# Filling a 1 MB DRAM scratch with 128 copies of a bias vector: from four SBUF partitions, or DRAM to DRAM with rows outermost

## Chip, core and metric

The kernel runs on one core of a Trainium2 chip. The metric is device time in microseconds (us) of one execution; lower is better.

## The reference, cut to what matters

Two networks of two layers each run one after the other on 256 tokens of width 1024 in fp32. The first block is a recurrent branch and a sliding-window attention, a cross attention and a SwiGLU feed-forward; the second is a differential attention beside a long convolution (Hyena). The part that this case touches is the position bias of the differential attention, which depends on the distance between key and query alone:

```python
bucket = t5_bucket(k_pos[None, :] - q_pos[:, None])      # 32 buckets
bias = rel_bias[bucket].astype(jnp.float32).transpose(2, 0, 1)   # 4 heads
logits = jnp.einsum('bhcqd,bhckd->bhcqk', q_blk, kt).astype(jnp.float32)
p = jax.nn.softmax(logits + bias[None, :, None], axis=-1)
```

## The kernel before

**The weight stream.** Almost all the work is `x @ w` with weights from DRAM. `run_stream` takes the weights in chunks of 1 MB. A chunk is loaded into one of three `raw` buffers (`NRAW`, L211, issued on SP's queue). Each chunk is used in two halves. A half is split into a high and a low part: ScalarE copies it to `wh` (L229) and VectorE subtracts to get `wl` (L231). The splits run four halves ahead of TensorE (`NW`). The matmuls (L361) of `fm` and `tm` take the split halves. A `raw` buffer is loaded again once its second half is split.

**The feed-forward (`ffn`).** In layer 1 of the first block it runs 11 rounds. A round takes two chunks of `ffn_wi` (matmuls into `fm`, then `silu` at L1004 and L1005) and one chunk of `ffn_wo` (matmuls into `ff`).

**Order of issue.** The program's order on TensorE and SP is written out by a planner in the file (`self.t`, the table `L`), which interleaves side chains between the halves of the weight stream. GpSimd (POOL) issues the small transfers in the chains' order.

**The bias chain (`load_bias`).** It is the tail of the chain `prep_co`, spawned just before the feed-forward of layer 1. One matmul of the bucket table with `rel_bias` gives, for each of the four heads, a vector of 512 values by distance, in four partitions (`vec`, L1224). POOL then writes 128 copies of it to a DRAM scratch `flat` (`scr`, L1226), 4 heads x 128 copies x 2 KB, 1 MB in all. Two POOL loads (L1232) read the scratch back with a row step of 511 instead of 512, so that each of the 128 partitions gets the vector shifted by one position (`bias`, 384 columns of two heads each). VectorE adds `bias` to the scores in `diff_co` (L1446) in the second block.

Of the kernel before, what the change touches and what calls it, by code (L numbers as in the profile page):

```python
# [13 lines left out]
F32 = mybir.dt.float32  # L14
# [6 lines left out]
P = 128  # L21
D = 1024
KD = D // P
S = 256
# [14 lines left out]
LATE = ((0, 0), (1, 0), (1, 1))  # filters whose products fill gaps of the tensor engine  # L39
# [5 lines left out]
# estimated time from the issue of a stage until its results are there, ns  # L45
# [10 lines left out]
def shape_constants():  # L56
    f32 = np.float32
    c = {}
    pos = np.arange(S, dtype=f32)
    inv = np.power(f32(500000.0), -np.arange(0, 16, 2, dtype=f32) / f32(16)).astype(f32)  # L60
    ang = (pos[:, None] * inv[None, :]).astype(f32).astype(np.float64)
    c["c_rope"] = np.concatenate([np.cos(ang), np.sin(ang)], axis=1).astype(f32)
    q = P + np.arange(P)[:, None]
    k = np.arange(S)[None, :]
    c["c_mask"] = np.where((k <= q) & (k > q - P), 0.0, NEG).astype(f32)
    # odd frequencies of length 2 S: g = f + 1/2 for f < P; those of 2 P - g follow from the
    # sums over even and odd positions
    t = np.arange(S).reshape(P, TB).T.reshape(TB, P, 1)
    th = 2.0 * np.pi * ((t * (2 * np.arange(P) + 1)) % 1024) / 1024.0
    fwd = np.concatenate([np.cos(th), -np.sin(th)], axis=2)  # L70
    c["c_fwd"] = np.ascontiguousarray(fwd.transpose(1, 0, 2)).astype(f32)
    c["c_inv"] = np.ascontiguousarray(
        fwd.reshape(TB, P, 2, P).transpose(3, 0, 2, 1)).reshape(P, TB, 2 * P).astype(f32)
    rel = np.arange(512) - 255
    n = np.abs(rel)
    large = np.full(512, 8)
    for edge in (12, 16, 23, 32, 46, 64, 91):
        large = large + (n >= edge)
    bucket = np.where(rel > 0, 16, 0) + np.where(n < 8, n, large)
    c["c_bucket"] = (np.arange(32)[:, None] == bucket[None, :]).astype(f32)  # L80
    tl = np.linspace(0.0, 1.0, S, dtype=f32)[:, None]
    fb = np.linspace(1e-4, 15, 16, dtype=f32)[None, :]
    za = (f32(2.0 * math.pi) * np.arange(S, dtype=f32)[:, None] * fb / f32(S)).astype(np.float64)
    z = np.concatenate([tl, np.cos(za), -np.sin(za)], axis=1).astype(f32)
    c["c_z"] = np.ascontiguousarray(z.reshape(P, TB, 33).transpose(2, 1, 0).reshape(33, S))
    c["c_nt"] = np.ascontiguousarray(-tl.reshape(P, TB))
    return c


class Chunk:  # L90
    """One weight transfer of [P, a, b], used in two halves (by column or by row)."""
# [12 lines left out]
class Net:  # L104
    def __init__(self, ctx, tc, a):
        self.tc, self.nc, self.a = tc, tc.nc, a
        self.const = ctx.enter_context(tc.tile_pool(name="const", bufs=1))
        self.wraw = ctx.enter_context(tc.tile_pool(name="wraw", bufs=NRAW))
        self.wspl = ctx.enter_context(tc.tile_pool(name="wspl", bufs=NW))
        self.slots = ctx.enter_context(tc.tile_pool(name="slots", bufs=NSLOT))  # L110
        self.sm = ctx.enter_context(tc.tile_pool(name="sm", bufs=2))
        self.ps = ctx.enter_context(tc.tile_pool(name="ps", bufs=4, space=PSUM))
        self.pa = ctx.enter_context(tc.tile_pool(name="pa", bufs=4, space=PSUM))
        self.dr = ctx.enter_context(tc.tile_pool(name="dr", bufs=1, space=bass.MemoryType.DRAM))
        self.n = 0
        self.first_hi = None
        self.start = True
        # splits of weights wait while a norm holds the vector engine, then queue behind .defer
        self.pause, self.defer = False, None
        self.t = 0.0  # L120
        self.chains, self.bg = [], []
        nc = self.nc
        self.ident = self.const.tile([P, P], F32, name="ident")
        make_identity(nc, self.ident)
        self.mhalf = self.const.tile([P, 4], F32, name="mhalf")
        nc.vector.memset(self.mhalf, -0.5)

    # ------------------------------------------------------------------ order of issue
    # Chains are generators that issue a stage and yield the time until the next one can start;
    # the weight stream runs between their stages.  # L130
# [14 lines left out]
    def pump(self):  # L145
        """issues the stages that are due"""
# [6 lines left out]
    def idle(self, until=None):  # L153
        """tensor engine has nothing to do: background stage, or let time pass"""
# [23 lines left out]
    def run_stream(self, gen):  # L178
        """items: Chunk, or a function to call when its turn comes"""
# [95 lines left out]
    def pin(self):  # L275
        """queues the block's work behind the latest split of weights"""
# [5 lines left out]
    # ------------------------------------------------------------------ tiles  # L282
# [10 lines left out]
    def fmt(self, name, n=2, dt=F32):  # L293
        """feature-major tensor, 4 chunks of [P, S] to a tile"""
# [27 lines left out]
    def tmp(self, shape, name="s", dt=F32):  # L322
        """short-lived: released by the stage that takes it"""
# [3 lines left out]
    def keep(self, shape, name="s", dt=F32):  # L327
        """lives over a few stages of a chain"""
# [19 lines left out]
    # ------------------------------------------------------------------ building blocks  # L348
# [26 lines left out]
    def fm(self, w, c0, ncols, x, evac, kc=KD):  # L375
        """chunks of x() @ w, feature-major; evac(pair, psum)"""
        step = 2048 // kc
        nm = step // 2 // P
        for c in range(c0, c0 + ncols, step):
            box = {}  # L380

            def half(h, wh, wl, c=c, box=box):
                xx = x()
                for i in range(h * nm, h * nm + nm):
# [4 lines left out]
                    # parts of one kind together: the others may still be on their way  # L389
# [16 lines left out]
    def tm(self, w, c0, ncols, x, evac):  # L406
        """chunks of x() @ w, token-major, 256 columns each; evac(chunk, block, psum)"""
        for c in range(c0, c0 + ncols, 256):
# [4 lines left out]
            def part(h, tb, wt, ps):  # L413
                xx = x()
                t = slice(tb * P, tb * P + P)
                if self.start:
                    # the lo part of the weights comes last
# [38 lines left out]
    def to_fm(self, src, x, scale=None):  # L456
        """chain: token-major [P, D] per block -> split feature-major x; gain and bias"""
# [31 lines left out]
    def load_x(self, src, name, n=1):  # L489
        """token-major loads, in n column parts"""  # L490
# [7 lines left out]
    # ------------------------------------------------------------------ block 1  # L498
# [58 lines left out]
    def ln_evac(self, t, h, n=256, f=1.0, gb=None, pause=False):  # L557
        """evac for tm: t = f * ALPHA * h + psum, psum being f times the branch, and its
        statistics; normalises a full block, with gain and bias if given"""
# [38 lines left out]
    def ln_co(self, l, i, t, hT):  # L598
        """chain: normalised t -> hT (split feature-major), then t *= gain, t += bias"""
# [8 lines left out]
    def swa_co(self, l, s):  # L608
        """chain: s.q, s.kv token-major -> s.ya feature-major split"""
# [111 lines left out]
    def conv4(self, l, s):  # L721
        """evac: stores the padded pair; a chain convolves it"""
# [23 lines left out]
    def gates(self, l, s):  # L746
        """chunks of the block-diagonal gate products"""
        nc, a = self.nc, self.a

        def half(h, which, wh, wl):  # L750
# [6 lines left out]
            # ig holds tanh(x / 2) = 2 sigmoid(x) - 1  # L757
# [22 lines left out]
    def rnn_co(self, l, s):  # L780
        """chain: gates r, ig and conv output xc -> hidden states times gelu(gr), split"""
# [19 lines left out]
        # the factor 1/2 of the input gate  # L801
# [23 lines left out]
    def merge(self, wa, wb, xa, xb, s, kc, before_b):  # L825
        """s.mg = 2 (sigmoid(a) * (xa @ wa) + sigmoid(b) * (xb @ wb)), feature-major split;
        s.sa, s.sb hold tanh(a / 2), tanh(b / 2) = 2 sigmoid - 1"""
# [26 lines left out]
    def mixer(self, l, s):  # L854
        """s.h, s.hT -> s.t (normalised token-major sums)"""
# [73 lines left out]
    def cross_co(self, s, hp):  # L929
        """chain: one head pair of cross attention up to transposed probabilities"""  # L930
# [41 lines left out]
    def cross_out(self, s):  # L972
        """attention-weighted values, feature-major split"""
# [93 lines left out]
    def block1(self, s):  # L1067
# [14 lines left out]
        for l in range(DEPTH):  # L1082
            last = l == DEPTH - 1
            # first half of the layer
# [58 lines left out]
    # ------------------------------------------------------------------ block 2  # L1143
    def load_block2(self):
# [16 lines left out]
        # the last layer's columns twice: the halves of its output take the hi and the lo part  # L1161
# [27 lines left out]
    def load_dft(self):  # L1189
        """transforms by parity of the position: [P, parity, cos | -sin], hi and lo"""  # L1190
# [13 lines left out]
    def dft_pair(self, part, src, alloc, name):  # L1204
        """cos (0) or -sin (1) sums of src over even and odd positions"""
# [8 lines left out]
    def load_bias(self):  # L1214
# [9 lines left out]
        nc.vector.tensor_copy(vec, ps)  # L1224
        flat = self.dr.tile([4, (P + 1) * 512], F32, name="scr")
        nc.gpsimd.dma_start(flat[:, :P * 512].rearrange("h (p r) -> h p r", r=512),  # L1226
                            vec[:, None, :].to_broadcast([4, P, 512]))
# [34 lines left out]
    def filter_piece(self, l, o, res):  # L1262
        """spectrum of the two-sided filter of order o, scaled for the inverse transform"""
# [86 lines left out]
    def filter_end(self, o, raws, res):  # L1350
        """sums and differences of the sums over even and odd positions"""
# [10 lines left out]
    def spectrum(self, u, flt, box):  # L1362
        """forward transform of u (token-major split [P, parity, 512]) times the filter's, as
        the operands of the inverse sums over even and odd positions"""
# [32 lines left out]
    def inverse(self, box, par, name):  # L1397
        """positions of one parity, token-major"""
# [29 lines left out]
    def diff_co(self, s, tb):  # L1428
        """chain: one query block of differential attention -> s.ya feature-major split"""
# [105 lines left out]
    def hyena_co(self, s, conv):  # L1535
        """chain: both long convolutions -> s.yh feature-major split"""
# [50 lines left out]
    def pre_co(self, l, s):  # L1587
        """chain: rms norm of s.x -> s.hT feature-major split"""
# [120 lines left out]
    def prep_co(self):  # L1709
        """chain: position biases and filters of block 2"""  # L1710
# [24 lines left out]
    def build(self, what, out):  # L1735
        """what: 1 or 2 for one block alone, 3 for both"""
# [45 lines left out]
```

## Time and profile before

| what | us |
|---|---|
| median of 3 runs | 1610.3 (1603.89 to 1612.5) |
| span of the profiled execution, first to last instruction (the only time given for it) | 1607.2 |
| TensorE busy in it | 1530.2 (95%) |
| mean granted TensorE clock in it | 0.978 |

All stretches are in microseconds from the start of the profiled execution's span. PE is TensorE's matmuls, DVE VectorE, ACT ScalarE, SPq the queue of the sync engine. [...] The transfers of one core run on 16 DMA engines; POOL's go through the queue q0, SP's through q1.

### The profile page before, as it was taken

How to read it: one execution, taken by the hardware profiler on the slowest of the kernel's cores; microseconds unless marked ns; L12 is line 12 of the kernel's file. 1: busy time of each engine (PE TensorE's matmuls, PEld its weight loads, DVE VectorE, ACT ScalarE, POOL GpSimd, SP SyncE). 2: the span in 40 equal slices, each digit the busy share in tenths (PEclk: the TensorE clock that was granted, in tenths of full speed). 3: DMA queues.
4: the chain of work that ended last, by engine and by line, in shares of the span. 5: the costliest groups of instructions: out<-in, count | busy, mean ns of one | idle time of the engine just before them, and what ended most of it. 6: DMA issues, size and time to landing. Idle time of an engine off the chain costs nothing. (4 is left out here: it accounts for less than half of the span.)

```text
span 1607.2 us, 28221 instructions
## 1 busy us (share of the span) xinstructions
PE 1530.2 (95%) x11740; PEld 1459.3 (91%) x11740; DVE 1135.2 (71%) x1646; ACT 879.3 (55%) x1406; POOL 138.1 (9%) x176
## 2 busy tenths in 40 slices
PE   8999999998999989999989899985999999999997
PEld 7889999998999989899989789975799899898997
DVE  5867677667664587767686776533798978797965
ACT  5789444534444446795446456622645565654753
POOL 5001002002000030010030210000000000000000
PEclk9999999999999999999999999996999999999999
DMA  8444654544555554446555375645454346354452
GB/s 274 132 132 146 223 185 157 172 156 157 165 178 187 186 165 134 130 145 211 196 162 192 105 236 186 202 119 171 131 162 158 123 141 197 132 163 157 133 170 79
DMA packets 228240, 263.10 MB, mean 164 GB/s; under 512 B 6367, under 2 KB 213497, under 8 KB 228112
## 3 DMA queue, kind: packets, MB, share of 16 engines
q1 hardware_dynamic: 221808, 246.43, 47.2%
q0 software_dynamic: 6304, 14.86, 3.8%
q8 instruction: 92, 1.51, 0.4%
q14 instruction: 36, 0.29, 0.1%
HBM read 259.17 MB, written 2.10 MB: 163 GB/s over the span
## 5 line engine op out<-in xcount | busy, mean ns | idle before, releaser
L231 DVE TENSOR_TENSOR wl<-raw,wh 128x1024 fp32r<-128x1024 f32 x464 | 570.1, 1232 | 312.0 <-ACT wh L229 309.2
L229 ACT ACTIVATE wh<-raw 128x1024 fp32r<-128x1024 f32 (+1 forms) x465 | 489.5, 1056 | 477.2 <-PE fm L361 271.3
L361 PE MATMUL fm<-h2h,wh 128*128 128x256 f32 x704 | 174.7, 289 | 25.0 <-ACT wh L229 23.8
L361 PE MATMUL fm<-h2l,wh 128*128 128x256 f32 x704 | 175.1, 290 | 9.9 <-DVE h2l L351 9.9
L361 PE MATMUL fm<-n2h,wh 128*128 128x256 f32 x640 | 176.6, 286 | 1.4 <-ACT n2h L350 1.4
L361 PE MATMUL fm<-n2l,wh 128*128 128x256 f32 x640 | 175.0, 284 | 0.0
L361 PE MATMUL fm<-n2h,wl 128*128 128x256 f32 x640 | 174.5, 283 | 0.0
L361 PE MATMUL fm<-h2h,wl 128*128 128x256 f32 x704 | 173.9, 288 | 0.5 <-DVE wl L231 0.5
L361 PEld LDWEIGHTS fm<-h2h,wh 128*128 128x128 f32 x704 | 126.9, 197 | 29.7 <-ACT wh L229 24.2
L361 PEld LDWEIGHTS fm<-h2l,wh 128*128 128x128 f32 x704 | 126.1, 198 | 11.5 <-DVE h2l L351 11.5
L361 PEld LDWEIGHTS fm<-h2h,wl 128*128 128x128 f32 x704 | 125.7, 197 | 0.8 <-DVE wl L231 0.8
L361 PEld LDWEIGHTS fm<-n2h,wh 128*128 128x128 f32 x640 | 119.9, 192 | 3.5 <-ACT n2h L350 1.9
L361 PEld LDWEIGHTS fm<-n2l,wh 128*128 128x128 f32 x640 | 119.8, 192 | 0.8 <-DVE n2l L351 0.8
L361 PEld LDWEIGHTS fm<-n2h,wl 128*128 128x128 f32 x640 | 119.9, 192 | 0.2
L361 PE MATMUL tm<-wh,mgl 128*128 128x256 f32 x256 | 72.5, 283 | 0.7 <-DVE mgl L351 0.7
L361 PE MATMUL tm<-wh,mgh 128*128 128x256 f32 x256 | 72.4, 283 | 0.0
L361 PE MATMUL tm<-wl,mgh 128*128 128x256 f32 x256 | 72.4, 283 | 0.0
L361 PE MATMUL fm<-h3h,wh 128*128 128x256 f32 x256 | 71.2, 288 | 0.0
L361 PE MATMUL fm<-xTh,wh 128*128 128x256 f32 x256 | 70.9, 287 | 0.0
L361 PE MATMUL fm<-h3l,wh 128*128 128x256 f32 x256 | 70.3, 285 | 0.0
L361 PE MATMUL fm<-h3h,wl 128*128 128x256 f32 x256 | 70.2, 284 | 0.0
L361 PE MATMUL fm<-xTl,wh 128*128 128x256 f32 x256 | 69.8, 283 | 0.0
(440 smaller groups left out, 4185.7 us busy)
## 6 DMA issues: line engine op xcount, KB each, us to landing
raw<-in_w_in_dram SPq DMA_DIRECT2D x89, 1024.0 KB, 5.3
raw<-in_ffn_wi_dram SPq DMA_DIRECT2D x44, 1024.0 KB, 5.1
raw<-in_ffn_wo_dram SPq DMA_DIRECT2D x22, 1024.0 KB, 5.0
raw<-in_w_out_dram SPq DMA_DIRECT2D x16, 1024.0 KB, 5.1
raw<-in_ckv_w_dram SPq DMA_DIRECT2D x16, 1024.0 KB, 5.2
raw<-in_w_br_attn_dram SPq DMA_DIRECT2D x8, 1024.0 KB, 5.1
raw<-in_w_br_rnn_dram SPq DMA_DIRECT2D x8, 1024.0 KB, 5.3
raw<-in_cq_w_dram SPq DMA_DIRECT2D x8, 1024.0 KB, 5.2
```

Of the source, the lines that this page charges most:

```text
L229: hi_ins = self.nc.scalar.activation(hi[:, i:i + q], s[:, i:i + q], AF.Copy)
L231: lo_ins = self.nc.vector.tensor_tensor(lo, s, hi.bitcast(F32), op=ALU.subtract)
L361: self.nc.tensor.matmul(out, lhsT=l, rhs=r, start=start, stop=stop)
```

## The change

The vector is first written once to a DRAM tile `one` (8 KB). The 128 copies are then made by a second transfer, also issued by POOL, from that tile to the scratch. Its access pattern has the 128 copies as the outermost dimension and the four heads inside; before, the four heads (partitions) were outermost. The contents of the scratch and all that reads it are the same.

```diff
         vec = self.tmp([512], "vec")[:4, :]
         nc.vector.tensor_copy(vec, ps)
+
+        one = self.dr.tile([4, 512], F32, name="row")
+        nc.gpsimd.dma_start(one, vec)
         flat = self.dr.tile([4, (P + 1) * 512], F32, name="scr")
-        nc.gpsimd.dma_start(flat[:, :P * 512].rearrange("h (p r) -> h p r", r=512),
-                            vec[:, None, :].to_broadcast([4, P, 512]))
+        nc.gpsimd.dma_start(flat[:, :P * 512].rearrange("h (p r) -> p h r", r=512),
+                            one[None, :, :].to_broadcast([P, 4, 512]))
```

The rest of the diff replaces comments and docstrings by blank lines.

## Rows read from the trace of the kernel before

**Rows 1.** The page: share of the span, and granted clock in 40 slices.

```profile
PE 1530.2 (95%) x11740; PEld 1459.3 (91%) x11740; DVE 1135.2 (71%) x1646; ACT 879.3 (55%) x1406; POOL 138.1 (9%) x176
...
PEclk9999999999999999999999999996999999999999
```

**Rows 2.** PE's waits, 1060 to 1260: in total, times, longest (us).

```profile
PE fm L361 <- ACT wh L229: 23.8, 1, 23.8
```

**Rows 3.** PE in order of time: start, duration, what, [idle before <- releaser].

```profile
1078.97 0.39 PE L361 MATMUL ff<-wh,al 128*128 128x512 f32 x1
1103.15 0.80 PE L361 MATMUL fm<-h2h,wh 128*128 128x256 f32 x2 [23.79 <-ACT wh L229]
...
1105.01 0.63 PE L361 MATMUL fm<-h2l,wh 128*128 128x256 f32 x2
...
1109.63 0.28 PE L361 MATMUL fm<-h2l,wh 128*128 128x256 f32 x1
```

**Rows 4.** ACT in order of time, the splits and the rounds' silu.

```profile
1069.13 0.58 ACT L1004 ACTIVATE silu<-fm 128x512 f32<-128x512 f32 x1
1102.04 2.00 ACT L229 ACTIVATE wh<-raw 128x1024 fp32r<-128x1024 f32 x2 [32.33 <-DMA raw<-in_ffn_wi_dram]
...
1113.42 0.58 ACT L1004 ACTIVATE silu<-fm 128x512 f32<-128x512 f32 x1
1115.34 1.06 ACT L229 ACTIVATE wh<-raw 128x1024 fp32r<-128x1024 f32 x1 [1.34 <-PE fm L361]
...
1130.40 0.58 ACT L1004 ACTIVATE silu<-fm 128x512 f32<-128x512 f32 x1
```

**Rows 5.** Two windows: length, busy by engine, clock, DMA share, GB/s.

```profile
1080.00:1090.00 10.00, 0.00 (x0) 0.00 (x0) 0.00 (x0) 0.00 (x0) 0.00 (x0) 0.61 0.25 31
...
1104.00:1108.00 4.00, 3.59 (x17) 3.59 (x18) 4.00 (x6) 2.57 (x4) 0.00 (x0) 0.50 0.71 261
```

**Rows 6.** DMA queues, 1072 to 1096: packets, MB, share of 16 engines.

```profile
q0 software_dynamic: 148, 0.61, 23.6%
q1 hardware_dynamic: 148, 0.15, 1.8%
```

**Rows 7.** DMA issues: count, KB each, us from issue to landing.

```profile
scr<-vec POOLq DMA_DIRECT2D x1, 1024.0 KB, 44.0
raw<-in_ffn_wi_dram SPq DMA_DIRECT2D x1, 1024.0 KB, 43.3
...
raw<-in_ffn_wi_dram SPq DMA_DIRECT2D x44, 1024.0 KB, 5.1
...
rb<-in_rel_bias_dram POOLq DMA_DIRECT2D x1, 0.5 KB, 2.9
```

**Rows 8.** SP's queue in order of time, from 1056.

```profile
1058.59 6.60 SPq L211 DMA_DIRECT2D raw<-in_ffn_wi_dram  x2
```

**Rows 9.** DMA queue, 1044 to 1050: weight loads alone.

```profile
q1 hardware_dynamic: 1231, 1.24, 64.0%
```

**Rows 10.** POOL in order of time, 1055 to 1150.

```profile
1057.73 1.13 POOL L1226 DMA_DIRECT2D scr<-vec  x1 [83.76 <-DVE vec L1224]
...
1147.00 1.00 POOL L454 TENSOR_TENSOR rs<-rs,mhalf 128x1 f32<-128x1 f32 x1 [43.27 <-DVE rs L450]
```

**Rows 11.** The use of bias: duration min/median/max, first and last start.

```profile
L1446 DVE SCALAR_TENSOR_TENSOR dsc<-ds,bias x16: 674/680/685, 1253.9 to 1513.8; 128x512 f32<-128x512 f32 x16
```

**Rows 12.** DMA, 924 to 930: POOL loads of DRAM rows copied to 128 partitions.

```profile
q0 software_dynamic: 278, 1.00, 61.3%
...
raw<-in_ffn_wo_dram SPq DMA_DIRECT2D x1, 1024.0 KB, 12.5
```

**Rows 13.** DMA queue, 1596 to 1604: stores of the output to DRAM.

```profile
q1 hardware_dynamic: 576, 1.05, 35.0%
```

**Rows 14.** All waits of PE, 915 to 960: total, times, longest.

```profile
PE fm L361 <- DVE h2l L351: 5.0, 4, 1.8
PE fm L361 <- ACT h2h L350: 1.2, 1, 1.2
```

## Prediction

> **What bounds the kernel now.** I read the page first. TensorE is busy 95% of the span and its granted clock is nine tenths or more in every slice but one, around 1085 to 1125, where it falls to six tenths [rows 1]. Almost everywhere the time is matmuls in a row, and nothing this change touches makes them shorter. So the question is what happens in that one slice, and whether the bias chain has to do with it.
>
> The waits of PE there hold one large entry: the first matmul of a round waits 23.8 us for `wh`, the high part of a weight half [rows 2]. In order of time, PE ends a round's `ff` matmuls at 1079.36 (1078.97 + 0.39) and starts again at 1103.15 [rows 3]. ACT, which makes `wh`, has waited since 1069.7 for a load of `ffn_wi` [rows 4]. So the wait is the weight stream's. Then the windows: in 1080 to 1090 no engine computes, yet the DMA share is 0.25, which is four of sixteen engines [rows 5].
>
> The queues say who holds the four. From 1072 to 1096 POOL's q0 sends 148 packets and SP's q1 148 packets, one for one [rows 6]. A q0 packet is 0.61 MB / 148 = 4 KB, two of the vector's copies, and takes 23.6% x 24 us x 16 / 148 = 0.61 us. A q1 packet is 1 KB of weights. A weight chunk has 64 such packets on each engine, so on each of these four it waits for 64 packets of q0, 64 x 0.61 = 39 us, while the other twelve engines have long done their part and sit idle. The issues agree: the copy lands after 44.0 us and the `ffn_wi` chunk issued beside it after 43.3 instead of the usual 5.1 [rows 7]. The reader should see two transfers of equal length here: the weights are slow because they alternate with the copy.
>
> **What the stall costs.** The rounds' `silu` at L1004 is a ruler with the same matmuls between its marks. From 1113.42 to 1130.40 a round takes 16.98 us; from 1069.13 to 1113.42 it takes 44.29 [rows 4]. The difference is 27.3 us. [...] I take 27.3.
>
> **The change, part by part.**
>
> *How late a chunk may be.* The delayed chunk was issued at 1058.59 [rows 8] and would land 5.1 us later [rows 7], at 1063.7. A `wh` split follows `silu` by 1.92 us (1115.34 - 1113.42), so it was wanted at 1071.05 [rows 4]. But splits run ahead of PE: PE began 1.11 us after the late split began (1103.15 - 1102.04), so a split begun by 1079.36 - 1.11 = 1078.25 costs PE nothing. The margin is 14.5 us. As a test, the old copy occupies four engines for 64 x (0.61 + 0.05) = 42.2 us, where 0.05 is a weight packet (64.0% x 6 x 16 / 1231 [rows 9]). One chunk gets through in that time, worth 16.98 / 3 = 5.7 us of PE's work: 42.2 - 5.7 - 14.5 = 22.0, against the 23.8 measured. The model holds within 2 us.
>
> *Removed:* 256 packets of 4 KB on four engines, and with them the stall.
>
> *Added, the row:* one more POOL transfer of 8 KB and a wait for it. POOL starts the old write at 1057.73 and has nothing of its own to compute before 1147 [rows 10]; behind the wait stand only the copy and the two bias loads. The bias is first read at 1253.9 [rows 11], some 150 us after it is ready now. The nearest row, a 0.5 KB POOL load, lands in 2.9 us [rows 7]. It costs POOL 3 to 5 us and PE nothing.
>
> *Added, the copy:* the same 1 MB, but with 128 outermost. If it spreads over 16 engines, each gets 16 packets. No row shows a transfer from DRAM to DRAM, so its packet is bounded. Above by the old copy: 0.61 us. Below by POOL loads that also repeat one DRAM row 128 times: 61.3% x 6 x 16 us for 1.00 MB, 0.24 us per 4 KB [rows 12]; a store to DRAM takes less, 35.0% x 8 x 16 us for 1.05 MB, 0.17 us per 4 KB [rows 13]. I take 0.24: same queue, same repeated source, no few partitions to read. It then runs 16 x (0.24 + 0.05) = 4.6 us, at most 10.6.
>
> What the old rows show of the source is 0.61 MB in 24 us, 25 GB/s over four engines [rows 6]. [...]
>
> *Moved:* the two bias loads start some 35 us earlier and now run beside weights in full flow: 0.77 MB, 12 packets an engine, 12 x 0.24 = 2.9 us. Together a weight chunk can lose 28 x 0.24 = 6.7 us, under the margin of 14.5. What hides it is the lead of three `raw` buffers and four split halves; without it the 6.7 us would show. That such a load is hidden can be seen earlier: beside those POOL loads a chunk took 12.5 us to land [rows 12], and PE had no wait for a weight there [rows 14].
>
> *The sum:* 1607.2 - 27.3 = 1579.9 for the span. The median of the runs shown is 3.1 us above the profiled span, so the time is **1610.3 - 27.3 = 1583.0 us**, a ratio of 0.983.
>
> **The rivals.**
>
> *A rest of the stall stays.* If the copy and the bias loads both cost 0.61 us a packet, a chunk loses 28 x 0.61 = 17.1 us, 2.6 over the margin: some 1586. Or the copy stays on four engines but at 0.24: 64 + 12 packets, 18.2 us, 3.7 over: some 1587. Against the first: only the four-partition copy shows such a packet.
>
> *Nothing changes.* The copy stays on four engines at 0.61 us, since the four heads are still a dimension of it, or the limit is the scratch's side and not the vector's: 1610. Against it: the stores [rows 13], and the order of the dimensions.
>
> *Slower: one engine takes it all.* Every POOL transfer in the trace has SBUF on one side, so that the spread follows partitions can't be excluded, and this copy has none. One engine then holds 256 packets: 256 x (0.24 + 0.05) = 74.2 us, in which four chunks pass, worth 22.6 us of PE: a stall of 74.2 - 22.6 - 14.5 = 37.1 us, 13.3 more than now, or **1623.6 us**. It decides from 0.22 us a packet on: below that the result is no slower by what can be told. Against it: the old copy used four engines for four partitions, which fits the outer dimension as well as partitions. [...]
>
> **How the numbers follow.** 1583 as forecast 0.80; a rest of the stall 0.12; nothing changes 0.05; slower 0.03. The measurement tells about 0.5% (8 us) from no change, so faster holds the first two, 0.92. The range takes in the rests, up to 1587, and the spread of the runs, 6.4 below and 2.2 above the median, with a little for a model that is off by 2 us: 1575 to 1591.
>
> **What the profile would show.** Right: no PE wait of more than a few us for `wh` in the feed-forward, `silu` marks about 17 us apart (18 in the round with the vector's matmul), no slice at half clock near 1100, a copy that lands in 5 to 11 us, and `ffn_wi` chunks beside it in under 15. Wrong, if a DMA share of 0.06 or 0.25 lasts for tens of us beside an idle PE, or if a wait for `raw` comes up with the bias loads. Wrong too, if ACT, DVE or POOL come out in another order and a new wait appears elsewhere; the rows of before can't show that.

## The result, and the profile after

The changed kernel takes 1580.47 us (median, 1579.31 to 1581.75) against 1611.39 us for the one before on the same chips: a ratio of 0.983 with a 95% interval of 0.980 to 0.9856. The two medians alone give 0.981; the four runs before spread from 1603.89 to 1612.5. Forecast were 1583.0 us and 0.983.

The profiled span went from 1607.2 to 1577.5 us, 29.7 us. They divide at the copy of the vector out of PSUM (`vec`, L1224, one instruction on VectorE), the first line from the trace of before, the second from the changed kernel's:

```profile
1056.75 0.68 DVE L1224 COPY vec<-vec 4x512 f32<-4x512 f32 x1 [0.26 <-PE vec L361]
...
1054.36 0.68 DVE L1224 COPY vec<-vec 4x512 f32<-4x512 f32 x1 [0.26 <-PE vec L361]
```

From its start to the end of the span it was 1607.2 - 1056.75 = 550.45 us, and is 1577.5 - 1054.36 = 523.14 us now: 27.3 us, the forecast sum. The other 2.4 us lie ahead of all that the change touches. Part of them can be seen in 660 to 680: PE is busy for 17.94 us in both executions, but gets through 130 matmuls at a granted clock of 0.91 before and 142 at 1.00 after. This isn't the change's doing: the first experiment below has the row too, and POOL begins to write it there at 1057.35, 2.0 us after the 1055.33 of the changed kernel.

The place of the stall in the changed kernel, first the waits of PE in 1040 to 1130 (all of them; in total, times, longest), then the two windows over it (length, PE, PEld, DVE, ACT, POOL, granted clock, DMA share, GB/s), then ACT's `silu` marks:

```profile
PE fd L361 <- ACT ft L1304: 0.2, 1, 0.2
```

```profile
1060.00:1070.00 10.00, 10.00 (x85) 10.00 (x85) 3.94 (x4) 4.73 (x5) 1.45 (x2) 1.00 0.93 316
1070.00:1080.00 10.00, 10.00 (x64) 9.04 (x63) 5.93 (x6) 3.79 (x5) 0.00 (x0) 1.00 0.58 204
```

```profile
1066.74 0.58 ACT L1004 ACTIVATE silu<-fm 128x512 f32<-128x512 f32 x1
...
1083.72 0.58 ACT L1004 ACTIVATE silu<-fm 128x512 f32<-128x512 f32 x1
...
1100.70 0.58 ACT L1004 ACTIVATE silu<-fm 128x512 f32<-128x512 f32 x1
```

The wait for `wh` of [rows 2] is gone, PE is busy through both windows at a granted clock of 1.00 where [rows 5] had nothing, and a round takes 16.98 us twice in a row where [rows 4] had one of 44.29. The copy now fills the DMA engines (0.93 in the first window instead of 0.25) for a short time, and the weights get through.

POOL's chain (start, duration, what, and what it waited for), the times from issue to landing, and the queues in 1060 to 1062:

```profile
1055.33 0.54 POOL L1227 DMA_DIRECT2D row<-vec  x1 [83.75 <-DVE vec L1224]
1057.35 0.79 POOL L1229 DMA_DIRECT2D scr<-row  x1 [1.49 <-DMA row<-vec]
1064.74 1.45 POOL L1235 DMA_DIRECT2D bias<-scr  x2 [6.60 <-ACT wh L229]
```

```profile
raw<-in_ffn_wi_dram SPq DMA_DIRECT2D x2, 1024.0 KB, 5.5
...
scr<-row POOLq DMA_DIRECT2D x1, 1024.0 KB, 6.9
bias<-scr POOLq DMA_DIRECT2D x2, 384.0 KB, 4.5
row<-vec POOLq DMA_DIRECT2D x1, 8.0 KB, 1.7
```

```profile
q0 software_dynamic: 151, 0.62, 78.8%
q1 hardware_dynamic: 205, 0.19, 28.3%
```

The copy lands 6.9 us after its issue instead of 44.0 [rows 7], and the weight chunks issued around it in 5.5 instead of 43.3. A 4 KB packet takes 78.8% x 2 us x 16 / 151 = 0.17 us instead of 0.61 [rows 6].

### The profile page after: what moved, and what is told of

Read it like the earlier page. It is cut to its first block, busy times and chain, and to the rows that moved or that the text cites. A ratio compares the mean times of both kernels' runs of the same rounds, so it can differ in the third digit from the quotient of the medians.

```text
span 1577.5 us, 28218 instructions
## 1 busy us (share of the span) xinstructions
PE 1525.3 (97%) x11740; PEld 1455.9 (92%) x11740; DVE 1135.1 (72%) x1646; ACT 880.8 (56%) x1406; POOL 138.1 (9%) x177
## 5 line engine op out<-in xcount | busy, mean ns | idle before, releaser
L229 ACT ACTIVATE wh<-raw 128x1024 fp32r<-128x1024 f32 (+1 forms) x465 | 490.5, 1058 | 450.5 <-PE fm L361 273.2
```

Of the source, the lines that this page charges most:

```text
L229: hi_ins = self.nc.scalar.activation(hi[:, i:i + q], s[:, i:i + q], AF.Copy)
```

## The experiments

The change does two things: the source becomes a DRAM row, and the outermost dimension becomes 128. The question is which of them pays, and why the old packet was slow. The theory to begin with: the four engines were tied up because each packet took 0.61 us. The rivals: that four engines hold the transfer at all, or that SBUF as a source does. Times are compared with the kernel before, run on the same chip; the changed kernel stands at 0.983 (0.980 to 0.9856).

**The DRAM row, with the heads outermost** (the changed kernel, with the order of before; code cuts are against the changed kernel where nothing else is said):

```diff
-        nc.gpsimd.dma_start(flat[:, :P * 512].rearrange("h (p r) -> p h r", r=512),
-                            one[None, :, :].to_broadcast([P, 4, 512]))
+        nc.gpsimd.dma_start(flat[:, :P * 512].rearrange("h (p r) -> h p r", r=512),
+                            one[:, None, :].to_broadcast([4, P, 512]))
```

> The copy still comes from the DRAM row, but with the four heads outermost, as in the kernel before. Theory (four engines matter only because each packet was slow: 0.61 us for 4 KB out of four partitions; in the changed kernel, packets from the DRAM row took 78.8% x 2 us x 16 / 151 = 0.17 us): four engines hold 64 packets each, 64 x (0.17 + 0.05) = 14 us, within the margin of 14.5; DMA share 0.25 for some 14 us, no wait of PE over 2 us, about 1581 us. Rival 1 (the count of engines decides, a packet stays at 0.6 us on four engines): a wait of some 24 us for wh, about 1608 us. Rival 2 (heads outermost do not confine a transfer between two DRAM tensors): the copy lands in 7 us as in the changed kernel, on 16 engines, and the time is 1581 too; the DMA share tells it from the theory.

Measured: 1579.94 us, ratio 0.982 (0.980 to 0.984). The copy's landing, and the queue in 1070 to 1074:

```profile
scr<-row POOLq DMA_DIRECT2D x1, 1024.0 KB, 15.8
```

```profile
q0 software_dynamic: 79, 0.32, 19.2%
```

The queue's share stays near a fifth and the copy takes 15.8 us, so it is confined to few engines as in the kernel before. A packet takes 19.2% x 4 x 16 / 79 = 0.16 us, and PE has no wait in the feed-forward beyond the 0.2 us shown above. Both rivals fall. The order of the dimensions is not what pays: with the source in DRAM, four engines are enough.

**Spread, but out of SBUF** (no DRAM row; `rb` is widened so that 32 partitions of each head hold the vector):

```diff
-        one = self.dr.tile([4, 512], F32, name="row")
-        nc.gpsimd.dma_start(one, vec)
...
+        for h in range(4):
+            nc.gpsimd.dma_start(flat[h, :P * 512].rearrange("(i c r) -> i c r", i=32, r=512),
+                                vec[h * 32:(h + 1) * 32, None, :].to_broadcast([32, 4, 512]))
```

> No DRAM row: the vector is made in all 128 partitions (32 for each head, by a wider matmul and one small DVE copy), and each partition writes 4 of the copies, in four transfers of 32 partitions. Theory (the fault of the kernel before is the four partitions, not that the source is SBUF): 16 engines, no wait for wh, about 1580 us, the same as the changed kernel within 0.5%. Rival (a source in SBUF that is read again and again is slow wherever it lies): packets of 0.6 us on 16 engines, 16 x 0.66 = 11 us, still hidden in time but to be seen in the packets' time; if it is slower still, a wait for wh comes back and the time lies between 1585 and 1611 us.

Measured: 1581.97 us, ratio 0.983 (0.9815 to 0.985). The four transfers, and the queue in 1058 to 1064:

```profile
scr<-vec POOLq DMA_DIRECT2D x4, 256.0 KB, 5.1
```

```profile
q0 software_dynamic: 254, 0.84, 65.1%
```

So the DRAM row isn't needed either: a copy spread out of SBUF does as well. The packet is not the fastest, 65.1% x 6 x 16 us for 0.84 MB or 0.30 us per 4 KB, but hidden. This is not the other half of the change by itself: along with the engines the source went from four partitions to 128. Sixteen engines reading the same four partitions were not tried.

**Four partitions, but not neighbours.** These two runs keep the write of before (heads outermost, each of the four partitions read 128 times) and only move the vectors to partitions 0, 4, 8, 12, or 0, 2, 4, 6 (the edit is against the kernel before; the wider matmul and `vec` are cut):

```diff
+        rw = self.tmp([4, 4], "rw")[:32]        # [4, 2] for 0, 2, 4, 6
+        nc.vector.tensor_copy(rw, rb[:, :, None].to_broadcast([32, 4, 4]))
...
         nc.gpsimd.dma_start(flat[:, :P * 512].rearrange("h (p r) -> h p r", r=512),
-                            vec[:, None, :].to_broadcast([4, P, 512]))
+                            vec[::4, None, :].to_broadcast([4, P, 512]))
```

> The write of the kernel before (no DRAM row, heads outermost, four engines, each engine reading one partition again and again), but the four vectors lie in partitions 0, 4, 8 and 12 instead of 0 to 3 (a wider matmul and one small DVE copy put them there). Theory (partitions 0 to 3 share one way into SBUF, and four engines queue at it, 25 GB/s together): on four ways a packet of 4 KB falls from 0.61 us to about 0.17, the copy lands in some 15 us as in the run with the DRAM row and heads outermost, no wait for wh, about 1580 us. Rival (reading one partition again and again is slow for each engine by itself): 0.61 us a packet, lands after 44 us, about 1608 us.

> As the run with partitions 0, 4, 8 and 12, but with partitions 0, 2, 4 and 6, two to a way if four neighbours share one. Theory: half the wait at each, 0.31 us a packet, 64 x (0.31 + 0.05) = 23 us for the copy, a wait of 23 - 5.7 - 14.5 = 3 us for wh, 1582 to 1587 us. Rival (each partition is slow by itself): 0.61 us a packet and 1608 us. Second rival (any four distinct partitions that are not neighbours are free): 0.17 us a packet, 1580 us.

Measured with a step of 4: 1580.54 us, ratio 0.983 (0.982 to 0.9845). With a step of 2: 1588.09 us, ratio 0.988 (0.986 to 0.990). Step 4, the landing and the queue in 1064 to 1068:

```profile
scr<-vec POOLq DMA_DIRECT2D x1, 1024.0 KB, 15.7
```

```profile
q0 software_dynamic: 80, 0.33, 19.9%
```

Step 2, the landing, the queue in 1070 to 1074, and PE's waits:

```profile
scr<-vec POOLq DMA_DIRECT2D x1, 1024.0 KB, 24.3
```

```profile
q0 software_dynamic: 48, 0.20, 22.1%
q1 hardware_dynamic: 48, 0.05, 3.5%
```

```profile
PE fm L361 <- ACT wh L229: 4.1, 1, 4.1
PE fm L361 <- DVE wl L231: 0.5, 1, 0.5
```

The packet takes 0.61 us from neighbours [rows 6], 22.1% x 4 x 16 / 48 = 0.29 with a step of 2, and 19.9% x 4 x 16 / 80 = 0.16 with a step of 4, as little as from DRAM. The read rate goes with it: 25 GB/s from partitions 0 to 3, 0.20 MB / 4 us = 50 GB/s from 0, 2, 4, 6, and 0.33 MB / 4 us = 82 GB/s from 0, 4, 8, 12. So the slow packet was no matter of reading a partition again and again, of SBUF, or of the scratch's side, which is the same in all three: it went with how close the four partitions lie. Why neighbours are slow together, no run shows, nor whether other partitions are.

**Half the copies the old way** (64 from the four neighbours, 64 from the DRAM row):

```diff
+        half = P // 2
+        nc.gpsimd.dma_start(flat[:, :half * 512].rearrange("h (p r) -> h p r", r=512),
+                            vec[:, None, :].to_broadcast([4, half, 512]))
+        nc.gpsimd.dma_start(flat[:, half * 512:P * 512].rearrange("h (p r) -> p h r", r=512),
+                            one[None, :, :].to_broadcast([half, 4, 512]))
```

> 64 of the 128 copies are written from the four partitions as before, the other 64 from the DRAM row with copies outermost. Theory (margin: weights alternate with packets of 0.61 us on four engines, and PE waits only for what exceeds 14.5 us): 32 x 0.66 = 21 us, less half a chunk that passes (2.8 us), less 14.5: PE waits some 4 us for wh, 1584 to 1587 us. Rival (the loss goes with the bytes that leave the four partitions): half of 27 us, about 1594 us, with a wait of 10 us or more.

Measured: 1586.32 us, ratio 0.986 (0.984 to 0.988). PE's waits in 1040 to 1130 (the two of them), and the queue in 1074 to 1078:

```profile
PE fm L361 <- ACT wh L229: 2.5, 1, 2.5
PE fm L361 <- DVE wl L231: 0.5, 1, 0.5
```

```profile
q0 software_dynamic: 26, 0.11, 24.2%
```

The packet is back at 24.2% x 4 x 16 / 26 = 0.60 us, the wait is 3 us and not half of 24: what counts is what exceeds the margin, not the bytes.

**Two engines** (the scratch with 8 KB for a copy, even and odd copies outermost):

```diff
+        flat = self.dr.tile([1, (P + 1) * 2048], F32, name="scr")
+        row = one.rearrange("h r -> (h r)")[None, :]
+        nc.gpsimd.dma_start(flat[0, :P * 2048].rearrange("(p q r) -> q p r", q=2, r=2048),
+                            row[:, None, :].to_broadcast([2, P // 2, 2048]))
...
+            src = flat[0:1, 127:127 + P * 2047].rearrange("o (p r) -> (o p) r", r=2047)
```

> The scratch is laid out with the four heads of a copy side by side (8 KB each) and the copies are split into even and odd ones, outermost, so that the slowest dimension of the DRAM to DRAM copy is 2; four bias loads instead of two. Theory (the slowest dimension says how many engines a transfer gets, whatever its source): two engines with 512 KB each, 128 packets of 4 KB, 128 x (0.17 + 0.05) = 28 us with a DMA share near 0.13; two chunks of weights pass (11.3 us); 28 - 11.3 - 14.5 = 2 us: a wait of 0 to 4 us, 1581 to 1586 us. Rival (a transfer between two DRAM tensors spreads anyway): lands in 7 us, 1581 us, no stretch at a share near 0.13. If a packet costs 0.24 us, as forecast: 37 - 11.3 - 14.5 = 11 us, about 1594 us.

Measured: 1587.83 us, ratio 0.987 (0.985 to 0.9885). The landing, the queue in 1078 to 1082, and PE's waits:

```profile
scr<-row POOLq DMA_DIRECT2D x1, 1024.0 KB, 26.1
```

```profile
q0 software_dynamic: 22, 0.18, 11.0%
```

```profile
PE fm L361 <- ACT wh L229: 2.7, 1, 2.7
PE fm L361 <- DVE wl L231: 0.8, 1, 0.8
```

The confinement is as expected: a queue share of 11%, under two engines of 16, and 0.32 us for a packet of 8 KB. The wait lies in the expected 0 to 4 us; the time is some 2 us over the expected range. In the profiled execution 7.1 us are lost behind the vector's copy against the changed kernel (from its start at 1056.0 to the end 530.3 us instead of 523.14): 5.4 in the two rounds at the wait, 3.5 of them waiting and the rest at a lower granted clock (the figures are given below), and 1.7 later. What took those is not shown.

**127 copies and one**, meant to put all on one engine, the prediction's slower rival:

```diff
+        nc.gpsimd.dma_start(flat[0, :127 * 2048].rearrange("(p r) -> p r", r=2048),
+                            row.to_broadcast([127, 2048]))
+        nc.gpsimd.dma_start(flat[0:1, 127 * 2048:P * 2048], row)
```

> The same scratch layout, with 127 copies in one transfer and the last in a transfer of its own: 127 has no divisor up to 16. Theory (the slowest dimension's divisors say how many engines): one engine with some 254 packets of 4 KB, 254 x (0.17 + 0.05) = 56 us at a DMA share near 0.06; four chunks pass (22.6 us); 56 - 22.6 - 14.5 = 19 us of waiting for wh, and some 3 us at the lower clock: about 1603 us. This is the slower rival of the prediction at the price of a packet since measured. Rival (127 copies are dealt out to 16 engines, 8 to each): lands in 7 to 9 us, 1581 us.

Measured: 1578.83 us, ratio 0.9815 (0.980 to 0.983). The two transfers' landings, and the queue in 1057 to 1062:

```profile
scr<-row POOLq DMA_DIRECT2D x1, 1016.0 KB, 7.4
...
scr<-row POOLq DMA_DIRECT2D x1, 8.0 KB, 7.1
```

```profile
q0 software_dynamic: 155, 1.02, 55.2%
```

My theory failed here: 127 has no divisor up to 16 but 1, yet the transfer holds 55.2% of 16 engines over 5 us, the time of 8.8 engines, and lands in 7.4 us. What decides the spread, and the share of each engine, is not shown. The one-engine case was thus not tried.

**No copy at all** (the bias is loaded straight from the row; the shift by partition is left out of the computation):

```diff
-            src = flat[hp * 2:hp * 2 + 2, 127:127 + P * 511].rearrange("h (p r) -> p h r", r=511)
-            nc.gpsimd.dma_start(b, src[:, :, 0:384])
+            nc.gpsimd.dma_start(b, one[None, hp * 2:hp * 2 + 2, 127:511].to_broadcast([P, 2, 384]))
```

> The copy and the scratch are left out: every partition of the bias gets the same 384 values straight from the DRAM row, so the shift by partition is left out of the computation. Theory (the copy is wholly hidden in the changed kernel): the same as the changed kernel, 1580 us within 0.3%. Rival (the copy and the wait for the row still cost something on the path): 2 to 5 us faster than the changed kernel.

Measured: 1580.81 us, ratio 0.982 (0.9805 to 0.984), the same as with the copy. So the copy in the changed kernel costs nothing that can be measured, and by these runs no other way of making it would be faster. The variants that leave no wait (row with either order, spread, step 4) can't be told apart.

## Why the prediction was right

**The stall's price.** 27.3 us, read from the `silu` marks, is what the span fell by behind the vector's copy, to a tenth. This term carried the whole sum. The time came 2.5 us under the 1583.0; nothing in the change accounts for that, and ahead of the vector the two profiled executions differ by 2.4 us.

**The margin of 14.5 us.** Shown right by the runs between the extremes, at the landing of the `ffn_wi` chunk issued beside the copy: half the old write, then a step of 2, then a step of 4:

```profile
raw<-in_ffn_wi_dram SPq DMA_DIRECT2D x1, 1024.0 KB, 22.1
...
raw<-in_ffn_wi_dram SPq DMA_DIRECT2D x1, 1024.0 KB, 23.7
...
raw<-in_ffn_wi_dram SPq DMA_DIRECT2D x1, 1024.0 KB, 15.0
```

Less the usual 5.1 us [rows 7] and the margin, the first two leave 2.5 and 4.1 us, the waits for `wh` measured in these runs. The third comes 4.6 us inside the margin, and PE doesn't wait.

**The 5.7 us for the chunk that passes.** Sized too large. With a step of 2 the working 64 x (0.29 + 0.05) - 5.7 - 14.5 gives 1.6 us of the 4.1 measured, as the test in the prediction gave 22.0 of 23.8. The chunk was late by 38.2 us (43.3 - 5.1) in the kernel before, where the prediction's formula holds the engines for 42.2, and by 18.6 with a step of 2, where it holds them for 21.8: 3 to 4 us come off, not 5.7. It didn't touch the sum, which took the stall from the marks.

**The copy's packet.** Taken at 0.24 us, between 0.17 and 0.61; measured 0.17. The term was 0.07 us too large, without effect, since it is hidden. The loads that it was taken from write into 128 partitions, the copy into DRAM; the store's 0.17 [rows 13] was the nearer row.

**The row and the bias loads.** The row cost POOL 2.0 us, from 1055.33 to 1057.35, instead of 3 to 5, and nothing waits for POOL. The bias loads, moved forward into the weights' flow, land in 4.5 us and PE has no wait from them. The lead of `raw` buffers and splits hides the rest: leaving the copy out altogether gains nothing.

**What the prediction had only half.** It counted the DRAM source (a cheaper packet) and the spread (16 engines) together. The runs show that the DRAM source alone removes the stall, on four engines; the spread does so too where the source is spread with it, and by itself it was not tried. What held the old write at 25 GB/s no row of before shows; with steps of 2 and 4 it was 50 and 82 GB/s, so it went with how close the four partitions lie. Of the rivals, "nothing changes" falls with the DRAM row and heads outermost: even on four engines the stall goes; with a step of 4 its other ground, a limit on the scratch's side, falls too. For four engines the prediction put a rest of 3.7 us at 0.24 us a packet; at 0.16 none is left. That 128 outermost would spread the copy no row of before shows, it was the author's estimate; in the changed kernel POOL's queue held 78.8% of the 16 engines in 1060 to 1062. "Slower: one engine" stays untried at its condition; at two engines the kernel is still faster than before. From 0.16 us a packet its own formula gives 256 x (0.16 + 0.05) = 54 us, 54 - 22.6 - 14.5 = 17 us of stall, an estimate, under the 24 of before.

## What to carry to other kernels

When an engine waits for weights and the DMA share sits at a round fraction such as 4/16 (0.25 here), ask which transfer holds those engines and compare its landing with the late one's: equal lengths (44.0 and 43.3 us here), and equal packet counts of the two queues (148 each), point to the two alternating. The write out of four neighbouring partitions was slow, 0.61 us for 4 KB; out of partitions four apart (0.16 us), spread over all 128 (0.30), or by a DRAM row (0.16 and 0.17) it was fast enough here; once the rest fits into the stream's lead, more speed there is worth nothing.

## What was not expected of the hardware

In these runs a short wait cost more than itself. Measured by the `silu` marks against 16.98 us, the waits of 3.0 us (half), 4.6 us (step of 2) and 3.5 us (two engines) lengthened the round by 6.2, 7.1 and 5.0 us (and with two engines the next round by 0.4). In order of time, ACT's marks of the half run:

```profile
1067.01 0.58 ACT L1004 ACTIVATE silu<-fm 128x512 f32<-128x512 f32 x1
...
1090.17 0.58 ACT L1004 ACTIVATE silu<-fm 128x512 f32<-128x512 f32 x1
```

and its windows around the wait:

```profile
1078.00:1082.00 4.00, 1.79 (x6) 1.50 (x7) 2.28 (x3) 2.42 (x3) 0.60 (x1) 0.70 0.25 90
1082.00:1086.00 4.00, 4.00 (x21) 4.00 (x20) 3.19 (x4) 2.22 (x3) 0.82 (x2) 0.50 0.85 287
1086.00:1090.00 4.00, 4.00 (x34) 4.00 (x33) 1.68 (x2) 1.85 (x2) 0.00 (x0) 0.94 1.03 299
```

The marks are 23.16 us apart. After PE's wait the granted clock is at 0.50 for all of the second window, in which PE issues 21 matmuls where the third has 34. The same happened after the long stall [rows 5]; there it was a ninth of the loss (27.3 us, of which PE waited 23.8 for `wh` and 0.5 for `wl`), here half (3.2 of 6.2). With a step of 2 the granted clock is 0.50 in 1078 to 1082 and 0.73 in 1082 to 1086, with two engines 0.78 in 1086 to 1090 and 0.79 in 1090 to 1094; there 2.5 of the 7.1 us and 2.0 of the 5.4 are not waiting.
